# Conditioning vectors on the vector engine: one multiply-and-add over K per 128 features, in place of eight scaled sums and a partition sum

## The chip, the cores and the metric

The kernel runs on one core of one Trainium2 chip. The metric is the device time of one execution in microseconds. Three runs of the kernel before gave 1397.26, 1393.45 and 1395.09 us, median 1395.09 us. The trace is of one profiled execution on that core.

## What is computed

A trunk of four layers works on x, 256 tokens of 1024 features, in float32. A conditioning vector c of 1024 elements turns into six modulation vectors of 1024 features for each layer:

```python
c_act = jax.nn.silu(c)
for i in range(DEPTH):
    mod = c_act @ ada_w[i] + ada_b[i]          # 1024 x 6144
    sh1, sc1, g1, sh2, sc2, g2 = jnp.split(mod, 6, axis=-1)
    h = modulate(rmsnorm(x, mix_norm_g[i]), sh1, sc1)
    y = mixer(h)                               # gMLP, attention, recurrence, gMLP
    x = x + (1.0 + g1)[:, None, :] * y
    h = modulate(rmsnorm(x, ffn_norm_g[i]), sh2, sc2)
    x = x + (1.0 + g2)[:, None, :] * conv_ffn(h, ...)
return rmsnorm(x, final_g)
```

Only the products `c_act @ ada_w[i]` (24 vectors, each with 4 MB of weights) are touched by the change; two of the 24 are made at the very start in another way.

## The kernel before, in words

x stays on chip with features on partitions, eight chunks of 128 features by 256 tokens. The weights of the big products are streamed from memory in units of 128 x 2048 float32 (1 MB) into tiles with the tag `raw`, of which there are five (`dma_next`, L168). Each unit is split in two halves: ScalarE copies 1024 columns to the high part `wh` (L200) and VectorE subtracts to get the low part `wl` (L201). TensorE then makes three products for each piece, high by high, high by low and low by high (`mm3`, L230 to L235). Activations are split in the same way (L450 and L451 for the normed input, L469 and L470 elsewhere).

The modulation vectors are worked in beside these products. `pacing` (L384), called once for each unit of weights, loads 1 MB pieces of `ada_w` at the rates of the table `RATE` and runs the work on pieces that were loaded two units earlier. `need` (L377) runs what is left when a norm or a residual step wants its vector. Nine vectors (`ADA_P`, L49) are made on TensorE by `ada_tensor` (L270) with the silu of c, repeated 32 times (`crep`, L154), as stationary operand. Thirteen vectors (`ADA_D`, L50) are made by `ada_vector` (L296) on VectorE: K lies on partitions there, 128 at a time. For a group of 512 features, eight instructions scale a 128 x 512 slice of weights by c for its eight K chunks and add it to `aacc`: one tensor-by-scalar (L311) and seven multiply-and-adds (L313). What is left is a sum over the 128 partitions. That is done by `end` (L315): four matmuls with a stationary operand of ones (L319), each into 32 partitions, and then `mod_store` (L253) transposes on VectorE (L256), takes one column, adds the bias (L258), and `mod_post` (L242) makes what the norms and residuals use (L249, L251). There is one `aacc` tile, so the next group's first step waits for the four matmuls. `end` is put on a list (`late`) and called one unit later (`ENDLAG`), behind the latest matmul of the main products (`issue_after(state["mm"])`):

```python
def end():
    ps = misc(f"adv{l}_{u}{g}", (P, P))
    with tc.issue_after(state["mm"]):
        for j in range(4):
            pe.matmul(ps[32 * j : 32 * j + 32, :], ones, t[:, P * j : P * j + P], start=True, stop=True,
                      tile_position=(0, 32 * j))
    mod_store(l, 8 * u + 4 * g, 4, ps[:])
```

Each matmul of float32 operands shows as two records in the trace, so the 26 groups of 512 features give 104 matmuls and 208 records.

The order of each engine's instructions is fixed when the kernel is built, by a list scheduler that goes by program order and by its own estimate of when operands are ready; at run time each engine's queue is worked through in that order. The start of the first layer has an order written out by hand (`FIRST`, L39): its steps `a` make the shift and scale of one feature chunk, `d` loads a unit of weights, `v` multiplies one K chunk, and `p` loads the bulk of the packed per-feature vectors `prm`. Weights, `prm` and `ada_w` pieces are all loaded on SyncE's queue. The last 737 columns of `prm`, most of them the taps and biases of the convolutions, are loaded by `late_consts` (L137) ahead of the first feed-forward block, where L1085 and L1086 read them.

Of the kernel before, what the change touches and what calls it, by code (L numbers as in the profile page):

```python
# [17 lines left out]
D = 1024  # L18
S = 256
L = 4  # L20
# [26 lines left out]
ENDLAG = 1  # L47
# [11 lines left out]
# columns of the packed per-feature vectors  # L59
_COLS = {}  # L60
_n = 0
for _name, _w in (("mix_g", 32), ("ada_b", 192), ("ffn_g", 32), ("final_g", 8), ("qg", 2), ("kvg", 1),
                  ("gmlb", 32), ("lb", 32), ("hgn", 1), ("cw", 528), ("cb", 176)):
    _COLS[_name] = _n
    _n += _w
# [27 lines left out]
def build(ctx, tc, A, out, stages=None):  # L93
# [74 lines left out]
    def dma_next():  # L168
# [13 lines left out]
    def conv_half():  # L182
        """the next 1024 elements a partition, to high and low parts"""
# [12 lines left out]
        with contextlib.ExitStack() as es:  # L196
            # a norm's short steps go first
# [27 lines left out]
    def hl(parts, o, n):  # L225
        """hi and lo views of elements o .. o+n of a unit"""
# [15 lines left out]
    def mod_post(l, b0, n):  # L242
        """what the blocks b0 .. b0+n of a layer's modulation vectors are used as"""
# [9 lines left out]
    def mod_store(l, b0, n, ps):  # L253
        """ps [128 = 4 j of 32 equal rows, (b, i)] to a column for each block b, feature 32 j + i"""
# [15 lines left out]
    def ada_tensor(l, u):  # L270
        """one of a layer's six modulation vectors on the tensor engine: four tiles of two K chunks"""

        def load(i):
# [3 lines left out]
            def run():  # L277
# [18 lines left out]
    def ada_vector(l, u):  # L296
        """the same on the vector engine: two groups of 512 features, two tiles of four K chunks each"""
        cur_ = {}

        def load(g, half):  # L300
            raw = ada_tile(f"adaw{l}_{u}_{g}{half}", (P, 4, 512))
            nc.sync.dma_start(raw[:].rearrange("p a b -> p (a b)"), A["adad"][ADA_D.index((l, u)), g, half])

            def run():
                if half == 0:
                    cur_[g] = tp.tile([P, 512], F32, tag="aacc", name=f"aacc{l}_{u}{g}", bufs=1)
                t = cur_[g]
# [20 lines left out]
        return [lambda g=g, h=h: load(g, h) for g in range(2) for h in range(2)]  # L328
# [3 lines left out]
    def ada_first(l, c):  # L332
        """shift and scale of one feature chunk of the mixer norm, all of K"""
# [3 lines left out]
        with contextlib.ExitStack() as es:  # L337
            if "pe" in firsts:
                es.enter_context(tc.issue_after(firsts["pe"]))
            for kc in range(KC):  # L340
                for j in range(4):
                    i = pe.matmul(ps[32 * j : 32 * j + 32, :], crep[:, kc, :], raw[:, kc, j, :], start=kc == 0, stop=kc == KC - 1,
# [34 lines left out]
    def need(l, u):  # L377
        """the modulation vectors of layer l up to the given one have to be done"""
# [5 lines left out]
    def pacing():  # L384
        """at each unit of weights: loads, and work on what was loaded two units before"""
# [40 lines left out]
    def square_chunk(c):  # L426
# [7 lines left out]
        if c == 0:  # L434
            # the table of square roots is loaded ahead of its use
# [36 lines left out]
    def pair(name, apart):  # L472
        """two accumulators, of one bank or of two"""
# [5 lines left out]
    def hilo(name, n):  # L479
        """hi and lo chunks [128, 256] of a matmul operand, eight to a tile"""  # L480
# [14 lines left out]
    def proj_pair(src_h, src_l, nk, name, outer=False):  # L495
        """two feature tiles of a unit with all of K, into one bank; K outermost where its chunks are still to come"""
# [16 lines left out]
    def proj_tok(blocks, name, sink, b0=0):  # L513
        """token-major products of h, 512 features at a time"""
# [14 lines left out]
    def proj_tok_first(name, sink, start=None):  # L529
        """the first 1024 features, K chunk by K chunk as h comes"""  # L530
# [31 lines left out]
    def gmlp(l, j, start=None):  # L562
# [11 lines left out]
        # the variance is taken about the mean of the first three quarters, and moved to the mean of all  # L574
# [726 lines left out]
```

## Time and profile before

| | |
|---|---|
| median of three runs | 1395.09 us (1393.45 to 1397.26) |
| profiled execution, first to last instruction | 1395.4 us |
| TensorE busy (matmul) | 1367.0 us, 98% |
| VectorE busy | 1111.0 us, 80% |
| ScalarE busy | 768.1 us, 55% |
| GpSimd busy | 16.8 us, 1% |
| memory read | 322.77 MB, 232 GB/s over the span |

The profiled execution's own time is its span, 1395.4 us, 0.3 us above the median of the three runs. Busy time of an engine is the union of its instructions; matmuls overlap one another, so the mean length of one is more than the distance from one to the next. The clock granted to TensorE was 0.996 of full speed over the span.

### The profile page before, as it was taken

What the parts mean: (1) busy time and instruction counts of PE and PEld (TensorE: products, weight loads), DVE (VectorE), ACT (ScalarE), POOL (GpSimd) and SP (SyncE); (2) the same over time, 40 slices, a digit from 0 to 9 for tenths busy, and PEclk for the clock granted to TensorE, in tenths of its full rate; (3) what the DMA queues carried; (4) which work ended last, traced back from release to release, by engine and by line L of the source; (5) the groups of instructions that cost most, each with busy time, mean ns of one, the idle gap of its engine ahead of it and who ended that gap; (6) DMA issues with size and microseconds to landing.
All of it is one profiled execution on the core that took longest, in us unless ns stands there. A gap on an engine that the chain in (4) does not pass through costs nothing.

```text
span 1395.4 us, 29809 instructions
## 1 busy us (share of the span) xinstructions
PE 1367.0 (98%) x12580; PEld 1290.1 (92%) x12580; DVE 1111.0 (80%) x1821; ACT 768.1 (55%) x1199; POOL 16.8 (1%) x17
## 2 busy tenths in 40 slices
PE   8999999999999999999998999999999999999997
PEld 6799999999887899999996999999987999999997
DVE  5799898898886698888888889899764964888853
ACT  3664366663455566654664646666355653666633
POOL 0100000000000000000000000000001000000000
PEclk9999999999999999999999999999999999999999
DMA  9868965558866266678576587558737465455531
GB/s 381 338 227 302 368 231 208 186 212 325 343 244 240 77 259 241 252 276 330 214 271 229 200 314 277 194 209 328 253 130 257 168 226 182 151 182 181 182 122 31
DMA packets 48765, 325.73 MB, mean 233 GB/s; under 512 B 5748, under 2 KB 8308, under 8 KB 11254
## 3 DMA queue, kind: packets, MB, share of 16 engines
q1 hardware_dynamic: 46848, 322.19, 61.8%
q8 instruction: 98, 1.61, 0.5%
q10 hardware_dynamic: 1784, 1.65, 0.4%
q14 instruction: 35, 0.29, 0.1%
HBM read 322.77 MB, written 1.05 MB: 232 GB/s over the span
## 4 chain that ended last, share of the span: by engine, by line
PE 92%; DMA 3%; DVE 2%; ACT 2%; issue 1%; DVEq 0%; SPq 0%; ACTq 0%
PE up L231 12%; PE up L232 12%; PE up L233 12%; PE dn L231 5%; PE dn L232 5%; PE dn L233 5%; PE go L231 2%; PE go L232 2%; PE go L233 2%; PE adaps L286 2%; PE v L231 2%; PE u L231 2%; PE u L232 2%; PE u L233 2%; PE v L233 2%; PE v L232 2%
## 5 line engine op out<-in xcount | busy, mean ns | idle before, releaser
L200 ACT CAST wh<-raw 128x1024 fp32r<-128x1024 f32 x426 | 434.7, 1031 | 389.2 <-PE up L232 157.1
L201 DVE TENSOR_TENSOR wl<-raw,wh 128x1024 fp32r<-128x1024 f32 x426 | 512.4, 1208 | 149.1 <-ACT wh L200 147.3
L231 PE MATMUL up<-hh,wh 128*128 128x256 f32 x1408 | 399.3, 285 | 2.6 <-ACT hh L450 2.5
L232 PE MATMUL up<-hlo,wh 128*128 128x256 f32 x1408 | 399.0, 284 | 0.0
L233 PE MATMUL up<-hh,wl 128*128 128x256 f32 x1408 | 399.0, 284 | 0.0
L231 PEld LDWEIGHTS up<-hh,wh 128*128 128x128 f32 x1408 | 270.6, 193 | 5.9 <-ACT hh L450 4.4
L232 PEld LDWEIGHTS up<-hlo,wh 128*128 128x128 f32 x1408 | 271.0, 193 | 0.4 <-DVE hlo L451 0.2
L233 PEld LDWEIGHTS up<-hh,wl 128*128 128x128 f32 x1408 | 271.1, 193 | 0.0
L231 PE MATMUL dn<-gh,wh 128*128 128x256 f32 x528 | 150.8, 286 | 0.0
L232 PE MATMUL dn<-gl,wh 128*128 128x256 f32 x528 | 149.6, 283 | 0.0
L233 PE MATMUL dn<-gh,wl 128*128 128x256 f32 x528 | 149.5, 283 | 0.0
L313 DVE SCALAR_TENSOR_TENSOR aacc<-adaw,cact,aacc 128x512 f32<-128x512 f32 x182 | 136.4, 749 | 1.5
L1088 ACT ACTIVATE y<-up,prm 128x256 f32<-128x256 f32 x176 | 98.6, 560 | 16.9 <-DVE y L1090 16.7
L231 PEld LDWEIGHTS dn<-gh,wh 128*128 128x128 f32 x528 | 101.3, 192 | 2.0 <-issue 1.6
L232 PEld LDWEIGHTS dn<-gl,wh 128*128 128x128 f32 x528 | 101.4, 192 | 0.0
L233 PEld LDWEIGHTS dn<-gh,wl 128*128 128x128 f32 x528 | 101.4, 192 | 0.0
L1090 DVE SCALAR_TENSOR_TENSOR y<-up,prm,y 128x254 f32<-128x254 f32 x176 | 84.6, 481 | 4.7
L1089 DVE SCALAR_TENSOR_TENSOR y<-up,prm,y 128x255 f32<-128x255 f32 x176 | 84.2, 478 | 1.5 <-ACT y L1088 1.4
L231 PE MATMUL u<-hh,wh 128*128 128x256 f32 x256 | 74.8, 292 | 0.0
L231 PE MATMUL go<-yh,wh 128*128 128x256 f32 x256 | 73.5, 288 | 0.0
L233 PE MATMUL u<-hh,wl 128*128 128x256 f32 x256 | 72.5, 283 | 0.0
L232 PE MATMUL u<-hlo,wh 128*128 128x256 f32 x256 | 72.5, 283 | 0.0
(339 smaller groups left out, 2510.9 us busy)
## 6 DMA issues: line engine op xcount, KB each, us to landing
raw<-up SPq DMA_DIRECT2D x88, 1024.0 KB, 4.8
adaw<-adad SPq DMA_DIRECT2D x52, 1024.0 KB, 7.5
adaw<-adap SPq DMA_DIRECT2D x36, 1024.0 KB, 6.9
raw<-dn SPq DMA_DIRECT2D x32, 1024.0 KB, 4.8
raw<-gmu SPq DMA_DIRECT2D x16, 1024.0 KB, 4.9
raw<-gmo SPq DMA_DIRECT2D x16, 1024.0 KB, 6.3
raw<-gmv SPq DMA_DIRECT2D x15, 1024.0 KB, 5.2
raw<-dn SPq DMA_DIRECT2D x16, 768.0 KB, 4.6
```

Source lines behind the costliest of these rows:

```text
L200: act.copy(wh[:, :w], raw[:, o : o + w])
L201: i = dve.tensor_tensor(wl[:, :w], raw[:, o : o + w], wh[:, :w].bitcast(F32), op=ALU.subtract)
L231: pe.matmul(ps, lh, rh, start=start, stop=False)
L232: pe.matmul(ps, lh, rl, start=False, stop=False)
L233: i = pe.matmul(ps, ll, rh, start=False, stop=stop)
L286: pe.matmul(ps[32 * j : 32 * j + 32, :], crep[:, kc, :], raw[:, k, j, :], start=kc == 0, stop=kc == KC - 1, tile_position=(0, 32 * j))
L313: dve.scalar_tensor_tensor(t[:], raw[:, k, :], cact[:, kc : kc + 1], t[:], op0=ALU.mult, op1=ALU.add)
L1088: act.activation(y[:], ps[:, e, :], AF.Identity, bias=b, scale=w[2])
L1089: dve.scalar_tensor_tensor(y[:, 1:], ps[:, e, : S - 1], w[1], y[:, 1:], op0=ALU.mult, op1=ALU.add)
L1090: dve.scalar_tensor_tensor(y[:, 2:], ps[:, e, : S - 2], w[0], y[:, 2:], op0=ALU.mult, op1=ALU.add)
```

## The change

`ada_vector` now lays features on partitions and K along the free dimension. A 1 MB piece holds two blocks of 128 features with all 1024 K values. For each block one `tensor_tensor_reduce` multiplies the weights by the silu of c (a tile `cbc` that holds the same 1024 values on every partition), writes the products over the weights, sums them along the free dimension starting from the bias, and writes the sum to the vector's column. There is no `aacc`, no matmul, no transpose and no bias step; `mod_post` runs once for a whole vector. `cbc` is loaded (512 KB) and put through silu on ScalarE in the first layer's start, at step `p`. `crep` is no longer copied out; the matmuls of `ada_tensor` and `ada_first` read the column of `cact` with a step of zero. The convolution's taps and biases leave `prm` and are loaded for each layer into a tile `cwb` (128 x 176) of two buffers: for the first layer at step `p`, for the others ahead of their mixer.

```diff
-ENDLAG = 1
-    crep = one.tile([P, 8, 32], F32, name="crep")
-    dve.tensor_copy(crep[:], cact[:].unsqueeze(2).broadcast_to([P, 8, 32]))
+    def crep(kc):
+        return cact[:, kc : kc + 1].broadcast_to([P, 32])
+    cbc = one.tile([P, D], F32, name="cbc")
+    def late_c():
+        with tc.issue_after(state["lastdma"]):
+            nc.sync.dma_start(cbc[:], A["cb"])
+        act.activation(cbc[:], cbc[:], AF.Silu)
...
-                        pe.matmul(ps[32 * j : 32 * j + 32, :], crep[:, kc, :], raw[:, k, j, :], start=kc == 0, stop=kc == KC - 1,
+                        pe.matmul(ps[32 * j : 32 * j + 32, :], crep(kc), raw[:, k, j, :], start=kc == 0, stop=kc == KC - 1,
...
     def ada_vector(l, u):
-        cur_ = {}
-        def load(g, half):
-            raw = ada_tile(f"adaw{l}_{u}_{g}{half}", (P, 4, 512))
-            nc.sync.dma_start(raw[:].rearrange("p a b -> p (a b)"), A["adad"][ADA_D.index((l, u)), g, half])
+        def load(i):
+            raw = ada_tile(f"adaw{l}_{u}_{i}", (P, 2, D))
+            nc.sync.dma_start(raw[:].rearrange("p a b -> p (a b)"), A["adad"][ADA_D.index((l, u)), i])
             def run():
-                if half == 0:
-                    cur_[g] = tp.tile([P, 512], F32, tag="aacc", name=f"aacc{l}_{u}{g}", bufs=1)
-                t = cur_[g]
-                for k in range(4):
-                    kc = 4 * half + k
-                    if kc == 0:
-                        dve.tensor_scalar_mul(t[:], raw[:, k, :], cact[:, kc : kc + 1])
-                    else:
-                        dve.scalar_tensor_tensor(t[:], raw[:, k, :], cact[:, kc : kc + 1], t[:], op0=ALU.mult, op1=ALU.add)
-                def end():
-                    ps = misc(f"adv{l}_{u}{g}", (P, P))
-                    with tc.issue_after(state["mm"]):
-                        for j in range(4):
-                            pe.matmul(ps[32 * j : 32 * j + 32, :], ones, t[:, P * j : P * j + P], start=True, stop=True,
-                                      tile_position=(0, 32 * j))
-                    mod_store(l, 8 * u + 4 * g, 4, ps[:])
-                if half == 1:
-                    late.append((state["use"] + ENDLAG, end, (l, u)))
+                for e in range(2):
+                    b = 8 * u + 2 * i + e
+                    c0 = col("ada_b", l * 48 + b)
+                    dve.tensor_tensor_reduce(raw[:, e, :], raw[:, e, :], cbc[:], 1.0, prm[:, c0 : c0 + 1], ALU.mult, ALU.add,
+                                             mod[:, l, b : b + 1])
+                if i == 3:
+                    mod_post(l, 8 * u, 8)
...
+    def conv_load(l):
+        convs[l] = tp.tile([P, 176], F32, tag="cwb", name=f"cwb{l}", bufs=2)
+        with tc.issue_after(state["lastdma"]):
+            nc.sync.dma_start(convs[l][:], A["cwb"][l])
...
             if not quick:
+                conv_load(l)
                 pace("mix", l, {0: 24, 1: 9, 2: 20}[l % 3], {0: "raw", 1: "big", 2: "raw"}[l % 3])
...
                             if step == "p":
                                 with tc.issue_after(state["lastdma"]):
                                     nc.sync.dma_start(prm[:, n0:n1], A["prm"][:, n0:n1])
+                                conv_load(l)
+                                late_c()
                                 continue
```

## Rows read from the trace of the kernel before

**Rows 1.** The page: the span, and busy time of each engine.
```profile
span 1395.4 us, 29809 instructions
PE 1367.0 (98%) x12580; PEld 1290.1 (92%) x12580; DVE 1111.0 (80%) x1821; ACT 768.1 (55%) x1199; POOL 16.8 (1%) x17
```
**Rows 2.** The page: the chain that ended last, by engine.
```profile
PE 92%; DMA 3%; DVE 2%; ACT 2%; issue 1%; DVEq 0%; SPq 0%; ACTq 0%
```
**Rows 3.** Groups by line, TensorE: busy us, mean ns, idle before and releaser.
```profile
L319 PE MATMUL adv<-aacc,ones 128*32 128x128 f32 x208 | 11.4, 284 | 0.8 <-DVE aacc L313 0.8
```
**Rows 4.** Timeline of TensorE at the first group's matmuls: start us, us.
```profile
92.83 0.28 PE L232 MATMUL u<-hlo,wh 128*128 128x256 f32 x1
92.95 0.28 PE L233 MATMUL u<-hh,wl 128*128 128x256 f32 x1
93.16 0.43 PE L319 MATMUL adv<-aacc,ones 128*32 128x128 f32 x8
93.52 0.38 PE L231 MATMUL u<-hh,wh 128*128 128x256 f32 x1
93.74 0.28 PE L232 MATMUL u<-hlo,wh 128*128 128x256 f32 x1
```
**Rows 5.** Timeline of TensorE at the second group's matmuls.
```profile
107.84 0.43 PE L319 MATMUL adv<-aacc,ones 128*32 128x128 f32 x8 [0.78 <-DVE aacc L313]
```
**Rows 6.** Groups by line and shape, VectorE.
```profile
L313 DVE SCALAR_TENSOR_TENSOR aacc<-adaw,cact,aacc 128x512 f32<-128x512 f32 x182 | 136.4, 749 | 1.5
L311 DVE TENSOR_SCALAR aacc<-adaw,cact 128x512 f32<-128x512 f32 x26 | 13.3, 512 | 7.4 <-PE adv L319 7.4
L256 DVE STREAM_TRANSPOSE adat<-adv 128x128 f32<-128x128 f32 x26 | 8.1, 311 | 4.8 <-PE adv L319 4.7
L258 DVE TENSOR_TENSOR mod<-adat,prm 128x4 f32<-128x4 f32 x26 | 4.1, 157 | 0.1
L201 DVE TENSOR_TENSOR wl<-raw,wh 128x1024 fp32r<-128x1024 f32 x410 | 501.5, 1228 | 138.5 <-ACT wh L200 136.7
L201 DVE TENSOR_TENSOR wl<-raw,wh 128x512 fp32r<-128x512 f32 x16 | 11.0, 685 | 10.6 <-ACT wh L200 10.6
```
**Rows 7.** Groups by line, ScalarE: reading a sum out of its accumulator.
```profile
L567 ACT ACTIVATION_READ_ACCUMULATOR v<-v 128x1 f32 x16 | 3.2, 200 | 0.0
```
**Rows 8.** Three stretches: us; busy PE, PEld, DVE, ACT, POOL; clock; DMA, GB/s.
```profile
69.80:104.70 34.90, 34.90 (x296) 34.30 (x295) 32.99 (x60) 21.36 (x30) 0.00 (x0) 1.00 0.64 228
104.70:139.50 34.80, 34.02 (x294) 33.32 (x294) 34.19 (x56) 15.43 (x20) 0.00 (x0) 1.00 0.82 302
627.90:662.80 34.90, 34.90 (x304) 34.01 (x303) 29.89 (x45) 14.29 (x19) 0.00 (x0) 1.00 0.84 330
```
**Rows 9.** The same stretches, instructions on `aacc` alone: PE, PEld, DVE.
```profile
69.80:104.70 34.90, 0.43 (x8) 0.16 (x8) 6.20 (x9) 1.00 0.64 228
104.70:139.50 34.80, 0.85 (x16) 0.34 (x16) 13.53 (x19) 1.00 0.82 302
627.90:662.80 34.90, 0.85 (x16) 0.31 (x16) 15.89 (x22) 1.00 0.84 330
```
**Rows 10.** The page: GB/s in 40 slices; timeline of SyncE's queue at step `p`.
```profile
GB/s 381 338 227 302 368 231 208 186 212 325 343 244 240 77 259 241 252 276 330 214 271 229 200 314 277 194 209 328 253 130 257 168 226 182 151 182 181 182 122 31
...
28.47 0.42 SPq L1181 DMA_DIRECT2D prm<-prm  x1
32.10 8.27 SPq L178 DMA_DIRECT2D raw<-gmv  x4
```
**Rows 11.** Timeline of ScalarE around the first gelu.
```profile
42.19 0.51 ACT L450 ACTIVATE hh<-nt,mod 128x256 fp32r<-128x256 f32 x1 [3.43 <-DVE nt L449]
42.60 1.99 ACT L200 CAST wh<-raw 128x1024 fp32r<-128x1024 f32 x2
44.60 1.28 ACT L567 ACT_TABLE_LOAD   x1
```
**Rows 12.** Waits of TensorE's weight loads: us in total, times, longest.
```profile
PEld v L231 <- ACT v L567: 1.4, 3, 0.5
```

More of the change, by code (lines that the diff above doesn't have):

```diff
@@ L62 @@
 for _name, _w in (("mix_g", 32), ("ada_b", 192), ("ffn_g", 32), ("final_g", 8), ("qg", 2), ("kvg", 1),
-                  ("gmlb", 32), ("lb", 32), ("hgn", 1), ("cw", 528), ("cb", 176)):
+                  ("gmlb", 32), ("lb", 32), ("hgn", 1)):
     _COLS[_name] = _n
@@ L296, in ada_vector @@
     def ada_vector(l, u):
-        cur_ = {}
-        def load(g, half):
-            raw = ada_tile(f"adaw{l}_{u}_{g}{half}", (P, 4, 512))
-            nc.sync.dma_start(raw[:].rearrange("p a b -> p (a b)"), A["adad"][ADA_D.index((l, u)), g, half])
+        def load(i):
+            raw = ada_tile(f"adaw{l}_{u}_{i}", (P, 2, D))
+            nc.sync.dma_start(raw[:].rearrange("p a b -> p (a b)"), A["adad"][ADA_D.index((l, u)), i])
             def run():
-                if half == 0:
-                    cur_[g] = tp.tile([P, 512], F32, tag="aacc", name=f"aacc{l}_{u}{g}", bufs=1)
-                t = cur_[g]
-                for k in range(4):
-                    kc = 4 * half + k
-                    if kc == 0:
-                        dve.tensor_scalar_mul(t[:], raw[:, k, :], cact[:, kc : kc + 1])
-                    else:
-                        dve.scalar_tensor_tensor(t[:], raw[:, k, :], cact[:, kc : kc + 1], t[:], op0=ALU.mult, op1=ALU.add)
-                def end():
-                    ps = misc(f"adv{l}_{u}{g}", (P, P))
-                    with tc.issue_after(state["mm"]):
-                        for j in range(4):
-                            pe.matmul(ps[32 * j : 32 * j + 32, :], ones, t[:, P * j : P * j + P], start=True, stop=True,
-                                      tile_position=(0, 32 * j))
-                    mod_store(l, 8 * u + 4 * g, 4, ps[:])
-                if half == 1:
-                    late.append((state["use"] + ENDLAG, end, (l, u)))
+                for e in range(2):
[5 more added lines that the diff above has]
+                    mod_post(l, 8 * u, 8)
             return run
-        return [lambda g=g, h=h: load(g, h) for g in range(2) for h in range(2)]
+        return [lambda i=i: load(i) for i in range(4)]
     firsts = {}
@@ L341, in ada_first @@
                 for j in range(4):
-                    i = pe.matmul(ps[32 * j : 32 * j + 32, :], crep[:, kc, :], raw[:, kc, j, :], start=kc == 0, stop=kc == KC - 1,
+                    i = pe.matmul(ps[32 * j : 32 * j + 32, :], crep(kc), raw[:, kc, j, :], start=kc == 0, stop=kc == KC - 1,
                                   tile_position=(0, 32 * j))
@@ L1070, in hgrn @@
             {"o": recur, "s": root, "n": normed, "w": wo.step, "a": lambda i: ada_run("p") if i < HGF else None}[step[0]](int(step[1]))
+    convs = {}
+    def conv_load(l):
+        convs[l] = tp.tile([P, 176], F32, tag="cwb", name=f"cwb{l}", bufs=2)
+        with tc.issue_after(state["lastdma"]):
+            nc.sync.dma_start(convs[l][:], A["cwb"][l])
     def ffn_units(l):
@@ L1084, in ffn @@
                 f = c + NF * e
-                w = [prm[:, col("cw", (l * 3 + i) * 44 + f) : col("cw", (l * 3 + i) * 44 + f) + 1] for i in range(3)]
-                b = prm[:, col("cb", l * 44 + f) : col("cb", l * 44 + f) + 1]
+                *w, b = (convs[l][:, i * 44 + f : i * 44 + f + 1] for i in range(4))
                 y = t1("y")
@@ L1142, in build @@
         nc.sync.dma_start(prm[:, n0:n1], A["prm"][:, n0:n1])
+        nc.sync.dma_start(cbc[:], A["cb"])
+        act.activation(cbc[:], cbc[:], AF.Silu)
     warm = misc("warmup", (P, P))
@@ L1242, in pack @@
         [cols(f[k]) for k in ("mix_norm_g", "ada_b", "ffn_norm_g", "final_g", "mla_q_norm_g", "mla_kv_norm_g", "gm_ln_b",
-                              "hg_lb", "hg_norm_g", "ff_conv_w", "ff_conv_b")], 1))
+                              "hg_lb", "hg_norm_g")], 1))
+    r["cwb"] = np.stack([np.concatenate([cols(f["ff_conv_w"][l]), cols(f["ff_conv_b"][l])], 1) for l in range(L)])
     aw = f["ada_w"]
@@ L1248, in pack @@
     r["adap"] = np.stack([ap[l, :, :, :, u].transpose(0, 2, 1, 4, 3, 5).reshape(4, P, 2048) for l, u in ADA_P])
-    ad = aw.reshape(L, 2, 4, P, 6, 2, 4, 4, 32)
-    r["adad"] = np.stack([ad[l, :, :, :, u].transpose(3, 0, 2, 1, 5, 4, 6).reshape(2, 2, P, 2048) for l, u in ADA_D])
+    r["adad"] = np.stack([np.ascontiguousarray(aw[l, :, u * D : u * D + D].T).reshape(4, 2, P, D).transpose(0, 2, 1, 3).reshape(4, P, 2048)
+                          for l, u in ADA_D])
+    r["cb"] = np.ascontiguousarray(np.broadcast_to(f["c"], (P, D)))
     r["ada0"] = np.ascontiguousarray(aw[:1, :, :2048].reshape(1, KC, P, 2, 8, 4, 32).transpose(0, 4, 2, 1, 5, 3, 6)).reshape(1, 8, P, 2048)
```

## The prediction

> **What bounds the kernel now.** I read the page first. TensorE is busy 1367.0 of 1395.4 us [rows 1], and the chain that ended last runs through TensorE for 92% of the span [rows 2]; the 8% that is left is DMA, VectorE, ScalarE and issue together. So TensorE's own work sets the time nearly everywhere, and the first question of any change here is how much time it takes out of TensorE's queue. VectorE is busy 80% on average [rows 1], which looks safe; but an average hides stages, so I looked at stretches of 35 us next. In the first feed of the gMLP it is busy 32.99 of 34.90 and then 34.19 of 34.80 us, and in the second layer's down product 29.89 of 34.90 [rows 8]. Those are the stretches in which dearer VectorE work could become the bound.
>
> **What is removed from TensorE.** 26 groups of four matmuls with a stationary operand of ones. Their row gives 11.4 us busy [rows 3], 0.44 us a group. But neighbouring matmuls overlap in these rows, so I take the cost from starts. Around the first group the last product starts at 92.95, the group at 93.16, the next two products at 93.52 and 93.74 [rows 4]. From 92.95 to 93.74 are 0.79 us. Without the group there would be two steps of one product each. One product follows another by 0.12 us (92.83 to 92.95, [rows 4]), so two steps take 0.24, and the group costs 0.79 - 0.24 = 0.55 us. The other groups that I looked at, nearly all 26, stand in the same way. 26 x 0.55 = 14.3 us. One group also held TensorE 0.78 us for its last sum [rows 5], the only such wait (0.8 in total, [rows 3]). Together 15.1 us, all on the path, because TensorE is the path. Bounds: 11.4 us (busy time alone) and 15.1 us.
>
> **What is removed from and put on VectorE.** Removed: 182 multiply-and-adds (136.4 us), 26 scalings (13.3), 26 transposes (8.1), 26 bias steps (4.1): 161.9 us busy, and waits of 7.4 us for the four matmuls to free `aacc` and 4.7 us for them to be transposed [rows 6]. Added: 13 x 8 = 104 reductions over 128 x 1024. No row shows this operation. From below: a plain two-operand step over 128 x 1024 takes 1.228 us [rows 6], 104 x 1.228 = 128 us. The old multiply-and-add over 512 takes 749 ns against 685 for the plain step [rows 6], so the second arithmetic step adds 0.06; and reading a sum out of an accumulator took 0.20 us on ScalarE [rows 7], about half of which lay beside the next step. I take 1.228 + 0.06 + 0.10 = 1.39 us, 104 x 1.39 = 145 us. From above: two cycles for each element. The plain step costs 1228 - 685 = 543 ns more for 512 more columns, so half rate would make it 1228 + 1086 = 2.31 us, 104 x 2.31 = 240 us. I take 1.39 because the nearest row, a multiply-and-add of two float32 streams in on-chip memory, runs at the plain step's rate. VectorE then loses about 17 us of work and is not the bound; by itself that gives TensorE nothing, since its queue hardly waited for it.
>
> [...]
>
> **What is added at the start.** At step `p`, 512 KB of `cbc` and 88 KB of `cwb` go into SyncE's queue behind `prm` (28.47 us) and ahead of the weight loads issued from 32.10 [rows 10]. At 338 GB/s, the rate of that slice [rows 10], 600 KB take 1.8 us, and every weight unit behind them lands that much later. TensorE pays between nothing (the units have been loaded ahead) and 1.8 us. ScalarE gets a silu over 1024 columns, about a cast's length (1.99 us for two, [rows 11]), and a table load of 1.28 [rows 11]: some 2.3 us. It sat idle 3.43 us before the step at 42.19 [rows 11]; if the scheduler puts the silu there it costs nothing. If it falls between 42.60 and the gelu, all of it goes to the gelus, and the next product waits for these to free its bank (waits of up to 0.5 us are there already, [rows 12]), so up to 2.3 us. Bounds 0 and 4.1 us; I take 1.5, since part of one of the two is likely to find room.
>
> **Costed at nothing.** Reading `cact` with a step of zero changes an address pattern, not the count of matmuls; and the copy that it saves is one step of VectorE of 256 columns, under 0.7 us by the plain step over 512 [rows 6], at a time when the first piece of `ada_w` is still being loaded. The convolution vectors are the same bytes as before, in four loads (on a queue that carries 1 MB pieces) in place of one. The in-place write lets a `raw` tile go after two instructions (2.8 us) instead of four (about 3.0), so no buffer is freed later. A reduction is 0.6 us longer than the step it replaces, and a short step of a norm can find itself behind it: with eight norms, 0 to 8 x 0.6 = 4.8 us; I take 0, since norms and residuals hold the old steps in the same places and the run now ends without a detour through TensorE.
>
> **Sum.** 1395.4 - 14.3 - 0.8 + 1.5 = 1381.8 us against the profiled span, which stands 0.3 above the median of the runs (1395.09); I give **1382 us**, 0.9% faster. A measurement of this kernel can tell about 0.3% (4 us) from no change.
>
> **Rivals.**
> *The reduction runs at half rate and VectorE becomes the bound.* In the three stretches `aacc` has 9, 19 and 22 instructions with 6.20, 13.53 and 15.89 us [rows 9]; half as many at 2.31 us are 10.4, 21.9 and 25.4, so 4.2, 8.4 and 9.5 us more, against idle time of 1.9, 0.6 and 5.0 us [rows 8]. What does not fit is 2.3 + 7.8 + 4.5 = 14.6 us. The 158 instructions elsewhere have more idle time around them; if they spill half as much, 7 us, that is 22 us: 1381.8 + 22 = 1404 us, slower by 0.6%. It decides from about 2.2 us an instruction on; at 2.0 us the three stretches spill 0.9 + 4.9 + 1.1 = 7 us and half the gain remains. [...] Against: the rate of every two-stream row. Chance 0.10.
>
> *The start and the coarser steps eat the gain.* All 4.1 us of the start and 4.8 us at the norms: 1395.4 - 15.1 + 8.9 = 1389 us. For it: the queues are in order, and the silu waits for a load that was issued late. Against: the idle 3.43 us, and DMA busy well below full in later slices. Chance 0.12, most of it still faster by over 0.3%.
>
> *The matmuls were hidden anyway*, that is, TensorE waits for weights or casts as soon as it runs ahead. Then only the start counts: 1395.4 + 1.5 = 1397, or 1394 with half of one stage's gain. Against: in all three stretches TensorE is busy for nearly the whole length while ScalarE is idle for 13 us and more [rows 8], so what feeds it has room. Chance 0.06.
>
> **How the numbers follow.** My forecast has 0.72. Its own range: 1395.1 - 15.1 = 1380 with nothing lost at the start, less 2 to 3 us for the spread of the runs (1393.45 to 1397.26) and another order of the queues, 1377; above, 1389 by the second rival, plus 2 for the spread, 1391. That leaves out half rate and the hidden case, 0.16 and some edge. Faster by over 0.3%: 0.72 + 0.11 and a little of half rate that comes out milder, 0.84; within 0.3%: 0.07; slower: 0.09.
>
> **What would show it.** Right: no matmul with ones in `ada_vector`, TensorE's busy time down by 11 us to about 1356, one group of 104 reductions at 1.2 to 1.5 us, VectorE's busy time near 1095 us, no transposes from `adv`, and waits of TensorE for VectorE no longer than before. Wrong: a reduction of 2 us or more and waits of TensorE for `wl`; or TensorE standing still for 3 us or more between 35 and 50 us, with ScalarE in the silu or in a table load.

## Result and profile after

| | before | after |
|---|---|---|
| median of four runs | 1395.55 us (1393.45 to 1397.26) | 1387.33 us (1385.15 to 1391.30) |
| ratio of the times, 95% interval | | 0.9946 (0.9934 to 0.9958) |
| profiled execution: span, own time | 1395.4, 1397.26 us | 1389.6, 1391.30 us |

The kernel is 0.54% faster, 7.5 us, where 13 us were forecast. One sentence of the text ahead of the prediction has to be put right first: the time of an execution is not its span. It stands 1.7 to 2.3 us above it in the runs here, and the profiled execution of before was the slowest of its runs (1397.26), not one at the median. The forecast does not hang on this: what was taken off, 13.6 us, gives 1381.5 from the median as well.

The page of the kernel after, span and TensorE's and VectorE's busy time (against [rows 1]) and the chain that ended last (against [rows 2]):

```profile
span 1389.6 us, 29284 instructions
PE 1358.8 (98%) x12372; PEld 1286.1 (93%) x12372; DVE 1091.6 (79%) x1760; ACT 770.8 (55%) x1201; POOL 17.2 (1%) x17
...
PE 92%; DVE 3%; DMA 3%; ACT 2%; issue 1%; DVEq 0%; SPq 0%; ACTq 0%
```

208 matmul records are gone, 8.2 us of TensorE's busy time and 19.4 us of VectorE's. The chain still runs through TensorE for 92%, but VectorE's share in it has gone up from 2 to 3%. The groups by line and shape, VectorE (busy us, mean ns, idle before and releaser), against [rows 6]:

```profile
L208 DVE TENSOR_TENSOR wl<-raw,wh 128x1024 fp32r<-128x1024 f32 x410 | 500.7, 1227 | 146.6 <-ACT wh L207 144.6
L315 DVE CUSTOM_DVE_ANT_0 adaw<-adaw,cbc,prm 128x1024 f32<-128x1024 f32 x104 | 131.3, 1276 | 2.2 <-DMA adaw<-adad 2.2
...
L315 DVE DVE_READ_ACCUMULATOR2_ANT mod<- 128x1 f32 x104 | 8.4, 81 | 0.0
```

The new reduction takes 1276 ns, as long as the plain two-operand step (1227) and 49 ns more, and its sum is read by an instruction of its own of 81 ns. The list of TensorE's waits (line, what it waited for, us in total, times, longest) has entries that the kernel before does not have; the longest three are:

```profile
PE psum L937 <- DVE hsg L953: 3.5, 1, 3.5
...
PE dn L238 <- ACT y L1089: 1.5, 1, 1.5
...
PE dn3b L240 <- DVE wl L208: 0.6, 1, 0.6
```

One is in the recurrence (`psum`), the others in the down products (`dn`, `dn3b`). To see where the gain went, I took the start of TensorE's first product of each stage, before and in a second execution of the unchanged kernel after (1388.74 us, experiment 1). "Forecast" is 0.55 us a group (0.78 more for the wait in the first feed), as the prediction had it, spread over the stages in which the 26 groups stood.

| stage, by its first product | groups removed | forecast, us | measured, us |
|---|---|---|---|
| start, up to `u` | 0 | +1.5 | +0.84 |
| first gMLP, `u` to first `up` | 6 | -4.08 | -4.29 |
| first up product | 0 | 0 | +0.17 |
| first down product, next norm | 4 | -2.20 | -2.47 |
| attention | 2 | -1.10 | +0.82 |
| second up product | 2 | -1.10 | -2.57 |
| second down product | 4 | -2.20 | -1.35 |
| recurrence, `hf` and `hq` | 1 | -0.55 | -0.53 |
| recurrence, `hi` to `o` | 1 | -0.55 | +1.43 |
| `o` to third up product | 2 | -1.10 | +0.20 |
| third up product | 1 | -0.55 | -0.53 |
| third down product | 3 | -1.65 | +0.15 |
| last layer | 0 | 0 | +0.07 |
| sum | 26 | -13.58 | -8.06 |

(The second up product has -1.08 in the profiled execution of after; the other 1.5 us differ between executions of one kernel.) So the first 375 us went as forecast, and from the attention on five stages gave back 7.9 us of what they should have won: attention 1.9, second down product 0.9, recurrence 2.0, `o` 1.3, third down product 1.8. These are figures of one execution each. The stage `hi` to `o` took 66.7 to 69.6 us in six traces that have the same wait in the recurrence (after, experiments 1, 5, 6, 8 and 10), by how long TensorE ran at half clock in it.

**The recurrence.** First SyncE's queue of the kernel after (start, us), then VectorE's timeline, then TensorE's:

```profile
696.17 10.73 SPq L185 DMA_DIRECT2D raw<-hg_i  x2
708.84 0.33 SPq L282 DMA_DIRECT2D adaw<-adap  x1
710.64 0.33 SPq L309 DMA_DIRECT2D adaw<-adad  x1
```

The first row merges two loads; in the list of the queue's waits between 690 and 716 us the longest is that of the second:

```profile
SPq L185 <- DVE wl L208: 14.0, 3, 10.0
```

```profile
715.76 0.68 DVE L953 TENSOR_TENSOR hsg<-hq,hk 128x512 f32<-128x512 f32 x1
718.65 1.28 DVE L315 CUSTOM_DVE_ANT_0 adaw<-adaw,cbc,prm 128x1024 f32<-128x1024 f32 x1 [2.22 <-DMA adaw<-adad]
719.86 0.08 DVE L315 DVE_READ_ACCUMULATOR2_ANT mod<- 128x1 f32 x1
719.86 1.22 DVE L208 TENSOR_TENSOR wl<-raw,wh 128x1024 fp32r<-128x1024 f32 x1
721.00 1.28 DVE L315 CUSTOM_DVE_ANT_0 adaw<-adaw,cbc,prm 128x1024 f32<-128x1024 f32 x1
...
722.21 1.22 DVE L208 TENSOR_TENSOR wl<-raw,wh 128x1024 fp32r<-128x1024 f32 x1
723.34 0.68 DVE L953 TENSOR_TENSOR hsg<-hq,hk 128x512 f32<-128x512 f32 x1
```

```profile
719.95 0.39 PE L238 MATMUL hi<-wh,hh 128*128 128x512 f32 x1
720.17 0.39 PE L239 MATMUL hi<-wl,hh 128*128 128x512 f32 x1
724.08 1.94 PE L937 MATMUL psum<-hsg,ones 128*32 128x512 f32 x8 [3.52 <-DVE hsg L953]
...
726.97 0.63 PE L239 MATMUL hi<-wl,hh 128*128 128x512 f32 x1
727.39 0.63 PE L240 MATMUL hi<-wh,hlo 128*128 128x512 f32 x1
```

A piece of `ada_w` is issued late, behind weights that waited 10.0 us for `wl` steps to free a buffer. The first of its two reductions stands at the head of VectorE's queue and waits 2.22 us for it; behind it in the queue are a `wl` step, the second reduction, another `wl` step and then the fourth `hsg` product, the fourth product of queries and keys. TensorE's sums of that product (L937) are next in its own queue, and it stands still for 3.52 us. The `hi` products then follow one another by 0.42 us where they had 0.23 before the pause. The stretches of 7 us around it (busy PE, PEld, DVE, ACT, POOL; granted clock; DMA, GB/s) tell why: the granted clock was 1.00 of full speed in the first and 0.51 in the second, and in shorter stretches 0.88 from 720.5 to 724.0 us and 0.50 from 724.0 to 729.0, so it was half from about the end of the pause on. The last line is the kernel before around its fourth `hsg` product (at 726.81), with TensorE busy throughout at full clock.

```profile
716.00:723.00 7.00, 4.56 (x26) 3.65 (x24) 4.78 (x7) 2.58 (x3) 0.00 (x0) 1.00 0.57 200
723.00:730.00 7.00, 5.92 (x18) 3.38 (x19) 5.04 (x6) 0.00 (x0) 0.00 (x0) 0.51 1.00 398
...
722.00:729.00 7.00, 7.00 (x46) 5.32 (x45) 5.77 (x7) 3.35 (x4) 0.00 (x0) 1.00 0.94 387
```

**The start.** ScalarE of the kernel after, against [rows 11]:

```profile
38.56 1.28 ACT L162 ACT_TABLE_LOAD   x1
39.85 1.06 ACT L162 ACTIVATE cbc<-cbc 128x1024 f32<-128x1024 f32 x1
42.31 0.51 ACT L444 ACTIVATE hh<-nt,mod 128x256 fp32r<-128x256 f32 x1 [1.41 <-DVE nt L443]
```

The table load and the silu fell into the idle time ahead of the step that stood at 42.19 before; that step is 0.12 us later.

### The profile page after: what moved, and what is told of

It reads as the page before. It is cut to its first block, busy times and chain, and to the rows that moved or that the text cites. A ratio compares the mean times of both kernels' runs of the same rounds, so it can differ in the third digit from the quotient of the medians.

```text
span 1389.6 us, 29284 instructions
## 1 busy us (share of the span) xinstructions
PE 1358.8 (98%) x12372; PEld 1286.1 (93%) x12372; DVE 1091.6 (79%) x1760; ACT 770.8 (55%) x1201; POOL 17.2 (1%) x17
## 3 DMA queue, kind: packets, MB, share of 16 engines
q10 hardware_dynamic: 1784, 1.65, 0.4%
HBM read 323.29 MB, written 1.05 MB: 233 GB/s over the span
## 4 chain that ended last, share of the span: by engine, by line
PE 92%; DVE 3%; DMA 3%; ACT 2%; issue 1%; DVEq 0%; SPq 0%; ACTq 0%
PE up L239 12%; PE up L238 12%; PE up L240 12%; PE dn L238 4%; PE dn L239 4%; PE dn L240 4%; PE go L238 2%; PE go L239 2%; PE go L240 2%; PE u L239 2%; PE u L238 2%; PE u L240 2%; PE adaps L293 2%; PE v L238 2%; PE v L239 2%; PE v L240 2%
## 5 line engine op out<-in xcount | busy, mean ns | idle before, releaser
L315 DVE CUSTOM_DVE_ANT_0 adaw<-adaw,cbc,prm 128x1024 f32<-128x1024 f32 x104 | 131.3, 1276 | 2.2 <-DMA adaw<-adad 2.2
L1089 ACT ACTIVATE y<-up,cwb 128x256 f32<-128x256 f32 x176 | 98.6, 560 | 10.1 <-DVE y L1091 9.8
L1091 DVE SCALAR_TENSOR_TENSOR y<-up,cwb,y 128x254 f32<-128x254 f32 x176 | 84.5, 480 | 4.7
L1090 DVE SCALAR_TENSOR_TENSOR y<-up,cwb,y 128x255 f32<-128x255 f32 x176 | 83.9, 477 | 0.8 <-ACT y L1089 0.8
```

Source lines behind the costliest of these rows:

```text
L315: dve.tensor_tensor_reduce(raw[:, e, :], raw[:, e, :], cbc[:], 1.0, prm[:, c0 : c0 + 1], ALU.mult, ALU.add, mod[:, l, b : b + 1])
L1089: act.activation(y[:], ps[:, e, :], AF.Identity, bias=b, scale=w[2])
L1090: dve.scalar_tensor_tensor(y[:, 1:], ps[:, e, : S - 1], w[1], y[:, 1:], op0=ALU.mult, op1=ALU.add)
L1091: dve.scalar_tensor_tensor(y[:, 2:], ps[:, e, : S - 2], w[0], y[:, 2:], op0=ALU.mult, op1=ALU.add)
```

## Experiments

Theory: TensorE's matmuls were removed at about the price forecast, and the coarser step of VectorE (1.28 us in place of 0.75) gave a part back, through steps that stand behind it in VectorE's queue. The rivals: the groups were worth less than 0.55 us, or the start took the difference. Later runs ask where the long step costs: at the late load in the recurrence, and at the `y` steps of the convolution that free the banks of the up product (D, where a letter is used). A bank here is the piece of accumulator memory that a product of TensorE is summed in; the planner is the list scheduler that fixes each engine's order when the kernel is built. Medians below come from several chips; each ratio is to the kernel before on the same chip.

**1. The kernel after, again** (no edit).

> The changed kernel as it is, once more. Theory A (the 26 groups took 14 to 15 us out of TensorE's queue, and about half came back as waits at a few places where the new order of the in-order queues has something late: the start, the recurrence, the down product of the third layer): 1385 to 1391 us again, with the same wait of about 3.5 us for the fourth product of queries and keys (tile hsg) in the recurrence. Theory B (each group costs the path less than 0.55 us, about 0.3): the same time. If the wait in the recurrence is an accident of one run, it is absent here and the time is 3 to 7 us less than 1391.

Measured: 1388.61 us (1386.98 to 1389.01), ratio 0.9941 (0.9924 to 0.9957). The wait for `hsg` is there again (2.7 us), so are the half clock behind it and the 1.5 us for `y`. The two waits belong to the kernel and not to one execution; the half clock behind the first does not come each time (experiment 8, last section).

**2. The kernel before without the matmuls of the groups.**

```diff
                 def end():
-                    ps = misc(f"adv{l}_{u}{g}", (P, P))
-                    with tc.issue_after(state["mm"]):
-                        for j in range(4):
-                            pe.matmul(ps[32 * j : 32 * j + 32, :], ones, t[:, P * j : P * j + P], start=True, stop=True,
-                                      tile_position=(0, 32 * j))
-                    mod_store(l, 8 * u + 4 * g, 4, ps[:])
+                    mod_store(l, 8 * u + 4 * g, 4, t[:, 0:P])
```

> The kernel before with VectorE's eight scaled sums, its transposes and its bias steps as they were, but without the 26 groups of four matmuls (the transposes read the unsummed tile, so the sum over partitions is left out). Theory A: 14 to 15 us off the kernel before, 1380 to 1382 us, since the work on VectorE and the loads are unchanged. Theory B: 7 to 8 us off, 1388 us.

Measured: 1383.85 us (1381.99 to 1385.02), ratio 0.9909 (0.9894 to 0.9923). Against the 1396.07 us of before on that chip the matmuls are worth 12.2 us, 0.47 us a group. The kernel after stands 1388.61 - 1383.85 = 4.8 us above this. Both figures are net of waits that moved: this kernel has two new ones in the first gMLP (1.0 us for `yh`, 1.2 for `hh`), and there it takes 2.7 us longer than experiment 1, while experiment 1 takes longer from `hi` to `o` (5.0 us), in the attention (1.1), the second and third down product (0.8 and 1.8) and at the start (1.1); from trace to trace that is 6.8 us.

**3. The kernel after with the matmuls put back**, on a constant operand.

```diff
+                def end():
+                    ps = misc(f"adv{l}_{u}{i}", (P, P))
+                    with tc.issue_after(state["mm"]):
+                        for j in range(4):
+                            pe.matmul(ps[32 * j : 32 * j + 32, :], ones, onesw[:], start=True, stop=True, tile_position=(0, 32 * j))
+
+                if i % 2:
+                    late.append((state["use"] + 1, end, (l, u)))
```

> The changed kernel with 26 groups of four matmuls of the old shape put back at the old places; they read constants and nobody reads them, so nothing waits for data. Theory A: 14.3 us more than the changed kernel (26 x 0.55), about 1401.5 us. Theory B: 7 to 8 us more, 1395 us.

Measured: 1401.66 us (1400.68 to 1402.06), ratio 1.0036 (1.0023 to 1.0049): 13.05 us over experiment 1, 0.50 us a group. This total is net as well: `hsg` is waited for 1.5 us here, without a half clock, and `hi` to `o` is 2.2 us shorter than in experiment 1. From both sides the groups cost 0.47 to 0.50 us net, and in the stages of the table that nothing else touched 0.53 to 0.54. The size of the forecast was 3 to 17% too high; that is at most 2 us and not the 5 that are missing. With the matmuls put back, the changed kernel is slower than the kernel before.

**4. The reduction at about half rate**: a product over 960 columns behind each reduction.

```diff
+                    dve.tensor_tensor(raw[:, e, :960], raw[:, e, :960], cbc[:, :960], op=ALU.mult)
```

> The changed kernel with one more VectorE step of 960 columns (about 1.06 us) behind each of the 104 reductions, so that each costs what half rate would cost, 2.3 us; the step writes to the piece of weights, which is not read any more. By the arithmetic of the prediction's first rival some 22 us are spilled onto TensorE: 1409 us. If VectorE's idle time can be used nearly everywhere (lists of work ahead of TensorE are long enough) it is under 10 us, below 1397.

Measured: 1443.29 us (1441.37 to 1446.78), ratio 1.0338 (1.032 to 1.0357). VectorE's busy time went from 1091.6 to 1199.0 us, 83% of the span, and of 107 us added, 1443.29 - 1388.61 = 55 came out at the end. TensorE's waits:

```profile
PE up L238 <- DVE y L1092: 11.9, 26, 1.3
PE dn L238 <- DVE y L1092: 6.6, 4, 2.0
PE bcn L416 <- DVE rsn L411: 4.6, 7, 1.3
```

The largest are not for the low parts `wl`, on which the first rival rested, but for `y`, the steps that read the up product out of its banks. VectorE was idle for a sixth of the time and still set it. Part of the 55 us is the clock: TensorE's was 0.981 over this execution, 0.995 in the kernel after, which comes to up to 20 us (an estimate, 0.014 of the span of 1445 us).

**5. No load of `cbc` and no silu**: GpSimd fills the tile with 0.5.

```diff
+    pool.memset(cbc[:], 0.5)
+
     def late_c():
-        with tc.issue_after(state["lastdma"]):
-            nc.sync.dma_start(cbc[:], A["cb"])
-        act.activation(cbc[:], cbc[:], AF.Silu)
+        pass
```

> The changed kernel with the tile of repeated conditioning values filled with a constant on GpSimd at the start: the 512 KB load and the silu of 1024 columns are left out (the thirteen vectors come out as plain weighted sums). Theory A: the first product of u starts 1.0 to 1.5 us earlier than in the changed kernel, near 69.6 us, and the end moves by the same 1 to 1.5 us, to 1386 to 1387. If the load and the silu were hidden: no difference (under 0.3 us at that place).

Measured: 1389.05 us (1387.76 to 1389.88), ratio 0.9945 (0.993 to 0.996), no faster than the kernel after. The first product of `u` starts at 70.55 us, against 70.69 with the load and 69.85 before. Between these two executions the load and the silu cost 0.1 us, but in the other kernels with the same start (after, experiments 6 to 12) `u` begins between 70.99 and 71.56 us, so a cost of up to 1 us is not excluded. The step that stood at 42.31 us in the kernel after stands at 42.18 here, so the silu itself is hidden, and the 0.7 us that the start is later even here than before have another cause.

**6. The reduction in two halves**: 512 columns each, the second starting from the sum of the first.

```diff
-                    dve.tensor_tensor_reduce(raw[:, e, :], raw[:, e, :], cbc[:], 1.0, prm[:, c0 : c0 + 1], ALU.mult, ALU.add,
+                    dve.tensor_tensor_reduce(raw[:, e, :512], raw[:, e, :512], cbc[:, :512], 1.0, prm[:, c0 : c0 + 1], ALU.mult, ALU.add,
+                                             mod[:, l, b : b + 1])
+                    dve.tensor_tensor_reduce(raw[:, e, 512:], raw[:, e, 512:], cbc[:, 512:], 1.0, mod[:, l, b : b + 1], ALU.mult, ALU.add,
                                              mod[:, l, b : b + 1])
```

> The changed kernel with each reduction cut in two of 512 columns, the second starting from the first one's sum: 208 steps of some 0.75 us and as many reads of the accumulator, about 20 us more for VectorE. Theory C (what is lost comes of the longer step, 1.28 us in place of 0.75, that short steps stand behind): the waits in the recurrence and at the third layer's down product shrink and the time falls by 3 to 5 us in spite of the added work, 1384. Theory A (order and late loads, whatever the length of the step): no gain; with half of the added 20 us on the path, as the run with dearer reductions showed, 1393 to 1399.

Measured: 1382.98 us (1380.85 to 1385.13), ratio 0.9902 (0.9883 to 0.9922), 5.6 us faster than experiment 1. Its groups, VectorE:

```profile
L317 DVE CUSTOM_DVE_ANT_0 adaw<-adaw,cbc,mod 128x512 f32<-128x512 f32 x104 | 76.4, 753 | 0.0
L315 DVE CUSTOM_DVE_ANT_0 adaw<-adaw,cbc,prm 128x512 f32<-128x512 f32 x104 | 76.0, 753 | 4.3 <-DMA adaw<-adad 4.3
```

152.4 us and twice the reads in place of 131.3: VectorE's busy time rises from 1091.6 to 1103.6 us, and the kernel is faster. The traced execution was the slowest of its four: in the traces TensorE's last product is 3.6 us earlier than in experiment 1, and the other 2 us are not located. From the down product's first product to the next norm it takes 54.81 us in the second and third layer, where experiment 1 has 55.62 and 56.58; the attention wins back 0.7 us. Halving did two things at once: it made the step shorter, and the planner put less reduction work ahead of the `y` steps (below, experiment 12). The wait for `hsg` in the recurrence stays (3.3 us), with the first half waiting 3.80 us for its load: that one is a matter of the late load and not of the step's length.

**7. No reduction ahead of the fourth product of the recurrence**: the rate of vector pieces there.

```diff
-        ("mix", 2): (0.05, 0.4),
+        ("mix", 2): (0.05, 0.5),
```

> The changed kernel with the rate at which vectors are loaded for VectorE ahead of the recurrence raised from 0.4 to 0.5, which moves the two reductions that stood in VectorE's queue ahead of the fourth product of queries and keys to other places. Theory A: TensorE's wait of about 3 us for that product is gone, and with it the 6.8 us at half clock that follow; from the first product of hi to the first of o it takes 64 to 66 us in place of 69, and the end is 3 to 5 us earlier, about 1384. If that wait has another cause (the load on ScalarE, the weights), it stays and the time with it.

Measured: 1385.62 us (1384.14 to 1386.27), ratio 0.992 (0.9905 to 0.9935). The wait is gone, `hi` to `o` takes 64.76 us (69.03 in experiment 1, which has 10.2 us at half clock in that stage; 66.67 in experiment 8, which has the wait and none), and `o` to the third up product, which I had not expected to change, 47.17 (49.04). The same stretches as above, in this kernel:

```profile
715.00:722.00 7.00, 7.00 (x46) 5.31 (x45) 4.57 (x5) 3.33 (x4) 0.00 (x0) 1.00 0.63 231
722.00:729.00 7.00, 7.00 (x37) 5.20 (x36) 6.65 (x10) 2.10 (x2) 0.00 (x0) 1.00 0.43 150
```

TensorE is busy throughout and keeps full clock.

**8. Reductions spread from the third down product over the up product ahead of it.**

```diff
-        ("up", 2): (0.0, 0.15), ("dn", 2): (0.1, 1.0),
+        ("up", 2): (0.0, 0.3), ("dn", 2): (0.1, 0.6),
```

> The changed kernel with the loads for VectorE's vectors of the last layer begun earlier and spread out (rate 0.3 in place of 0.15 in the third layer's up product, 0.6 in place of 1.0 in its down product). Theory A: TensorE's wait of 1.5 us at the start of the third down product goes, 1.5 to 1.8 us off the changed kernel, about 1387, unless the spread work makes a new wait among the up products. If the wait is one for weights or for ScalarE's own work it stays.

Measured: 1397.34 us (1395.83 to 1399.62, ten runs), ratio 1.0012 (1.0002 to 1.0022), 0.1% slower than the kernel before. The edit was meant to relieve the place and did the opposite. TensorE's timeline:

```profile
919.86 0.35 PE L238 MATMUL up<-hh,wh 128*128 128x256 f32 x1 [1.49 <-ACT y L1089]
926.24 0.35 PE L238 MATMUL up<-hh,wh 128*128 128x256 f32 x1 [0.40 <-DVE y L1091]
932.62 0.36 PE L238 MATMUL up<-hh,wh 128*128 128x256 f32 x1 [0.40 <-DVE y L1091]
```

Four reductions between 906 and 919 us make `y` late once, and from there every unit of the up product (6.38 us apart, 5.76 without a wait) waits for it again, up to the first product of the down product, which waits 1.42 us. The third up product takes 133.9 us in place of 126.8.

**9. Halves, and the rate of experiment 7** (both edits).

> Two edits together: each reduction in two steps of 512 columns, and the rate of 0.5 ahead of the recurrence. If the two gains are separate (the longer step at the up and down products, the order in the recurrence), they add up: 1383 less some 3 us, 1379 to 1381. If both came of the same place, no better than the better one alone, 1383.

Measured: 1380.12 us (1379.71 to 1383.6), ratio 0.9895 (0.9879 to 0.9912): 1.05% faster than before, and twice the gain of the change. The page:

```profile
span 1378.4 us, 29496 instructions
...
PE 1352.5 (98%) x12372; PEld 1282.1 (93%) x12372; DVE 1105.4 (80%) x1968; ACT 770.9 (56%) x1201; POOL 16.4 (1%) x17
```

The two gains add: TensorE's last product is 8.6 us earlier than in experiment 1 (3.6 with the halves alone, 3.6 with the rate alone, and 1.5 of the latter's was lost to the second up product's spread between executions).

**10. Other places for the reductions at the third down product.**

```diff
-        ("up", 2): (0.0, 0.15), ("dn", 2): (0.1, 1.0),
+        ("up", 2): (0.0, 0.0), ("dn", 2): (0.1, 1.2),
```

> The changed kernel, all eight pieces of VectorE's vectors for the last layer loaded during the third layer's down product (rate 0 in place of 0.15 in its up product, 1.2 in place of 1.0 in its down product). Theory D (a reduction of 1.28 us standing among the steps that free the up product's banks is what holds TensorE at the start of the down product): that wait of 1.5 us goes, 1.5 to 2 us off, about 1386.5. Theory E (the down product's own burst of reductions holds it): more of them there, so 1 to 4 us more, 1390.

Measured: 1386.36 us (1384.8 to 1387.25), ratio 0.9931 (0.9911 to 0.995). The wait for `y` is gone and the third down product takes 54.81 us to the norm. The edit does less than its name says: the planner draws reductions of the down product's pieces forward, and six stand between 944 and 963 us. But behind the product's start only four stand among the `y` steps, where the kernel after has eight.

**11. All three: halves and both rates.**

> All three edits together. By theory D with halves the third is worth nothing more (steps of 0.75 us do not hold the banks): as the two edits together, 1379 to 1381. By theory E 1 to 4 us more than these.

Measured: 1379.99 us (1379.19 to 1381.73), ratio 0.9889 (0.9872 to 0.9905), the same as experiment 9. With halves there is nothing left to win at the third down product.

**12. The down products in the order of the program.** In the kernel after, the planner's order has some products of the last pair of outputs (`dn3b`) ahead of their turn in the second and third down product; with halves it has the program's order. So the order could be the cause, and not the step. The reductions keep their length.

```diff
-                        mm3(pss[i][g], a, b, gh(kc), gl(kc), kc == 0 and (g == 0 or i == 3), kc == NF - 1 and (g == 1 or i == 3))
+                        with tc.issue_after(state["mm"]):
+                            mm3(pss[i][g], a, b, gh(kc), gl(kc), kc == 0 and (g == 0 or i == 3), kc == NF - 1 and (g == 1 or i == 3))
```

> The reductions keep their length of 1.28 us; only TensorE's order in the four down products is held to that of the program (each product issued behind the one before). In the kernel after, the planner had drawn products of the last output pair ahead in the second and third down product, where the stages took 55.63 and 56.58 us from the first down product to the next norm; in the kernels with halves the order was the program's and both took 54.81. If TensorE's order, made from the planner's estimates, is what costs there, both stages take about 54.8 us, the wait for y goes, and the time falls by 0.8 + 1.8 = 2.6 us to about 1386. If the long step itself is (a bank that is freed late, whatever the order), the third down product still waits 1.5 us for y, its stage stays near 56.5 us, and the time stays near 1388.6.

Measured: 1391.52 us (1390.37 to 1395.12), ratio 0.9974 (0.9961 to 0.9987). Neither number came: the two stages got longer, 58.7 and 61.2 us. TensorE in the third down product, and VectorE ahead of its second wait:

```profile
968.11 0.36 PE L238 MATMUL dn<-gh,wh 128*128 128x256 f32 x1 [1.49 <-ACT y L1089]
976.23 0.36 PE L238 MATMUL dn<-gh,wh 128*128 128x256 f32 x1 [2.14 <-DVE y L1091]
984.35 0.36 PE L238 MATMUL dn3a<-gh,wh 128*128 128x256 f32 x1 [1.14 <-DVE y L1091]
```

```profile
974.01 0.48 DVE L1090 SCALAR_TENSOR_TENSOR y<-up,cwb,y 128x255 f32<-128x255 f32 x1
974.40 1.28 DVE L315 CUSTOM_DVE_ANT_0 adaw<-adaw,cbc,prm 128x1024 f32<-128x1024 f32 x1
975.60 0.09 DVE L315 DVE_READ_ACCUMULATOR2_ANT mod<- 128x1 f32 x1
975.60 0.48 DVE L1091 SCALAR_TENSOR_TENSOR y<-up,cwb,y 128x254 f32<-128x254 f32 x1
```

The down product begins 23 us before VectorE has read the last of the up product out of its banks, and each new pair of outputs waits for a bank behind a `y` step that stands behind a reduction. So TensorE's order falls as a cause: the products drawn forward had hidden most of the delay. The planner moved something else too: in this kernel no reduction stands between the third and the fourth `hsg` product, TensorE does not wait there, and `hi` to `o` takes 64.80 us, as in experiment 7, with the rate unchanged. Without that the time would have been some 4 us longer (an estimate from the 69.03 us of experiment 1). The traces give the delay itself: the last `y` step on VectorE after the down product's start, beside the stage's length.

| kernel | second layer: last `y`, stage, us | third layer: last `y`, stage, us |
|---|---|---|
| before, each stage with 3 groups | 11.6, 56.4 | 12.0, 56.4 |
| halves (6) | 15.9, 54.8 | 13.1, 54.8 |
| other places in the third layer (10) | 20.5, 55.6 | 14.7, 54.8 |
| after, again (1) | 20.5, 55.6 | 23.0, 56.6 |
| program order (12) | 20.5, 58.7 | 23.0, 61.2 |

Up to 16 us nothing is lost (54.8 and three groups at 0.54 us are the 56.4 of before); from 20 on it is. Experiments 7 and 8 fit in the third layer: 21.4 us with a stage of 56.8, 21.8 with one of 59.0. What makes `y` late is the work on conditioning vectors that starts between the down product's start and that last step: in the second and third layer 2.2 and 1.2 us before, 7.7 and 10.2 in experiment 1, 5.2 and 4.5 with halves, and 5.1 in the third layer of experiment 10, whose reductions have their full length. (In experiment 8 it is 3.8: there the delay was made in the up product already.) So how much of it stands ahead of the `y` steps is shown to matter; that the length of a single step matters apart from this is not shown.

## Why the prediction came out as it did

The time lies inside the range, and the sign and the mechanism are right: TensorE is the path, and its matmuls came off it. The forecast of 13 us came to 7.5; what kept it in the range is the upper bound, taken from the second rival. Of the signs of being right, TensorE's busy time fell by 8.2 us and not 11, and the last one failed: TensorE does wait longer for VectorE than before. By its own steps:

- **What is removed from TensorE**: right in kind. 14.3 us were 12.2 (taken out alone) to 13.1 (put back), 0.47 to 0.50 us a group with the waits that moved, 0.53 to 0.54 without, where I had 0.55 from one place. The 0.78 us wait went too (the first gMLP won 4.29 us, forecast 4.08).
- **VectorE's reduction**: 1.39 us was forecast and 1.276 with a read of 0.081 came, so 139.7 us for the 145 of the sum. VectorE's busy time is 1091.6, forecast 1095. No run shows the half rate of the first rival: at that rate the row would show some 2.3 us (1.228 + 1.086, the author's bound from [rows 6]), and it shows 1.276.
- **The start**: of 1.5 us for the load and the silu, experiment 5 shows 0.1, with a spread of the start that leaves room for up to 1; the silu found the idle slot [rows 11] that I had named as the lower bound. The start came out 0.8 to 1.4 us later; 0.7 of that, by experiment 5, is something else, which stays open. The bound of 1.8 us for the load took 338 GB/s, the rate of the slice from 35 us on; the queue's 28.47 to 32.10 us lie in the first slice, at 381, so it is 1.6.
- **Costed at nothing, the coarser step: this is the term that failed.** I bounded it at 4.8 us and took 0, "since norms and residuals hold the old steps in the same places". It cost about 5 net: the kernel after stands 4.8 us above the kernel before without matmuls (the start among it, with 1.1 in the traces), and halves (5.6 us by the medians, 3.6 in the traces) or other places in the recurrence (3.0) bring it back. The new steps did not hold the places of the old: in the third down product the planner put 10.2 us of them ahead of the `y` steps where 1.2 had stood. I looked at the norms, and they fell on two other steps that TensorE waits for: the fourth `hsg` product, behind a reduction whose load was late, and the `y` steps that free the up product's banks. For each I had the lines in the trace; I did not ask which short steps of VectorE release TensorE.
- **The rival of half rate** was priced at 22 us by idle time in stretches of 35 us. Experiment 4, with 1.28 + 1.16 = 2.44 us a block, lost 55 us, up to 20 of them by the clock. The idle time of VectorE is no room for more work where it lies between steps that TensorE is waiting for.
- **The rival "the start and the coarser steps eat the gain"**, 1389 us, is nearest to the result; most of what was lost were the coarser steps, but at the places above and not at the norms.

What the runs show of the loss: the recurrence (experiment 7, with its late load and its half clock) and the two down products (6, 10 and 12). Open is the attention, of whose 1.9 us halves win back 0.7, and the 0.8 us at the start.

## What to carry to other kernels

Taking work off the bounding engine pays in full only where the work that replaces it leaves the other queues' short steps in place; before costing a longer instruction at nothing, list the steps behind it in its queue that release the bounding engine (a bank, a tile, an operand), not only those that are known to be short. Where such steps are close, keep the long instructions from piling up ahead of them: cutting each in two did that here, though it cost busy time. Put none whose load may be late ahead of them. An engine that is idle for a fifth of the time may still have no room.

## What the runs showed of the hardware

A stretch of experiment 12, right behind its second wait, then two of experiment 8, behind its pause of 3.53 us for `hsg` and behind one of 2.14 us in the third down product (columns as in the stretches of the kernel after):

```profile
976.00:983.00 7.00, 6.77 (x64) 6.22 (x64) 7.00 (x13) 3.20 (x5) 0.00 (x0) 1.00 0.93 312
...
723.00:730.00 7.00, 7.00 (x39) 4.54 (x39) 5.73 (x6) 1.05 (x1) 0.00 (x0) 1.00 0.88 353
974.00:977.30 3.30, 3.30 (x17) 3.30 (x17) 3.30 (x8) 0.41 (x1) 0.00 (x0) 0.50 1.00 422
```

- A pause of TensorE can cost more than itself, and its length alone does not tell whether it will. Behind the wait for `hsg` in the recurrence the granted clock was half for 6.8 us in the kernel after and in experiment 1 (pauses of 3.52 and 2.74 us), for 3.4 us in experiments 5, 6 and 10 (2.62, 3.27 and 3.02 us), and full in experiment 8 (3.53 us). Behind the same pause of 2.14 us in the third down product it stayed full in experiment 12 and was half for 3.4 us in experiment 8. Removing the pause of 2.7 us in experiment 7 shortened the stage by 4.3 us; against experiment 8, without half clock, it was 1.9.
- Reading the accumulated sum on VectorE is an instruction of its own, 81 ns in the row, and the step behind it mostly starts at the same time (85 of the 104 in the kernel after; in the other 19 it starts 0.07 to 3.08 us later, released by TensorE or ScalarE); on ScalarE the same kind of read took 200 ns [rows 7].
- The reduction runs at the rate of the plain step: 1276 ns for 1024 columns and 753 for 512, so 523 ns for 512 more columns, against 543 for the plain step [rows 6].
